# Adaptive-norm weights of the attention layer in 1 MB tiles of four row chunks, with their four products side by side

## The chip, the core and the metric

The kernel runs on one core of one Trainium2 chip. The metric is the device time of one execution in microseconds; the median of three runs of the kernel before is 3498.79 us (3496.82 to 3501.25).

## The reference, cut to what matters

Two blocks of two layers each are computed on 512 tokens of 1024 features, with 256 context tokens in the first block. In the first block every layer is steered by an adaptive norm:

```python
mod = jax.nn.silu(c) @ ada_w[i] + ada_b[i]            # [1, 6144]
sh1, sc1, g1, sh2, sc2, g2 = jnp.split(mod[:, None, :], 6, axis=-1)
mod_c = jax.nn.silu(c_ctx) @ ada_w[i] + ada_b[i]      # the same for the context
h = modulate(x, norm_mix_g[i], sh1, sc1)              # rmsnorm * (1 + sc) + sh
x = x + g1 * y                                        # y: attention (layer 0) or SSM (layer 1)
x = x + g2 * swiglu(modulate(x, norm_ffn_g[i], sh2, sc2), ...)
```

`ada_w` is [2, 1024, 6144] in float32, 24 MB a layer, and only two vectors (c and c_ctx) are multiplied with it.

## The kernel before, in words

The program is written for a tile framework: tiles come from pools with a fixed number of slots per tag, the framework sets all semaphores and orders each engine's instructions once, when the program is built, by their place in the program ("name@n" in an order gives way to n instructions) and by when they are expected to be ready. On the chip each engine then runs its list in that order.

**The adaptive norm.** `ada()` (line 434) makes 512 columns of mod at a time from `adal` (line 428), which holds silu(c) and silu(c_ctx) as two of 32 columns, for each of the eight row chunks. For chunk k it loads a [128, 512] tile `adaw` (256 KB, line 444, on the queue of SP) and multiplies (line 446): the 32 result rows go to the PSUM partitions 32 * (k % 4) and on, so chunks 0 to 3 write four different groups of 32 columns of the array, and chunks 4 to 7 add to the same four. Each such product in float32 is two MATMUL records in the trace. A copy by ACT (line 450, tile `adas`), four transposes on PE (line 452) and two short DVE instructions (lines 455 and 456) then give the columns in `mod`.

**Where it is called.** Tiles 0 to 3 of layer 0 are made at the start, two tiles at a time (phase "pre", 512 KB loads, eight slots). The other 20 tiles (line 2203, `rest`) are fillers of the attention of layer 0: `fill(n)` (line 2205), five for each of the four groups of heads, stands in the order `K["attn"]` as F.0 to F.4 between the steps Sc, S (scores and softmax), Vc, V (products with the values), P (preparing the next group's keys and queries) and o (output projection):

```python
rest = [(0, i) for i in range(4, 12)] + [(1, i) for i in range(12)]
def fill(n):
    l, i = rest[n]
    self.ada(l, [i], self.mod[l], (v1["ab0"], self.v2["ab1"])[l])
with self.side_pool("attnb") as ap:
    O = self.attn0(ap, op, qkv, xT, cT, m(2, 0), m(2, 1), fill)
```

`adaw` has six slots of 2 KB a partition there (`K["ada_w"]`, line 76), in the pool of the phase "attn". The pool "attnb" is opened at the other end of the memory, on the side where the pool of the normed activations `hx` and `hc` is closed just before (line 2200), with the pool "O" ahead of it; it holds the softmax's tiles `prob` (line 803). When attention is done it is closed, and `last_norm()` (line 2229) opens the pool of its tiles `h` on the same side.

**Other work beside it.** In a head group PE makes scores (lines 789, 790, 828, 830, 832), transposes of the exponentials (870), products with the values (883) and the turned reciprocals (895); DVE takes maxima (792, 850) and splits (312); ACT makes exponentials (799, 853) and splits (311). With the last group PE also makes the output projection's last part (lines 320 to 322, `g<-O,kwh`). SP's queue also loads the other weights (`wraw`, line 268), in the order of the list.

Of the kernel before, what the change touches and what calls it, by code (L numbers as in the profile page):

```python
# [9 lines left out]
F32 = mybir.dt.float32  # L10
# [18 lines left out]
# Choices: orders of issue, engines, numbers of slots and PSUM banks. In orders: steps "name", "name:lag" (of the group that many later) and "name@n" (gives way to n instructions).  # L29
# [46 lines left out]
    "ada_w": (6, 8),  # L76
# [29 lines left out]
class Act:  # L106
    """Feature-major activations split exactly into hi + lo: lists of [128, n] operands per chunk."""
# [5 lines left out]
class RmsStat:  # L113
    """Mean of squares of a token's features, gathered as the chunks [128, n] of x become final."""
# [33 lines left out]
class Gen:  # L148
# [11 lines left out]
    @contextmanager  # L160
    def phase(self, name, nc2, banks=(4, 2, 0, 0)):
        """A pool of one phase: nc2 general slots of [128, 512] and what else the phase allocates;
        banks: see banked()."""
        with self.tc.tile_pool(name=name, bufs=1, reuse_waits="tile") as p, ExitStack() as st:
            old = getattr(self, "ph", None), getattr(self, "nc2", 0)
            self.ph, self.nc2 = p, nc2
            if banks:
                st.enter_context(self.banked(name, *banks))
            yield p
            self.ph, self.nc2 = old  # L170

    @contextmanager
    def banked(self, name, *banks):
        """banks: slots of the PSUM tags "ps" (one bank), "ps2" (two banks), "S" and "F" (one bank)."""
# [7 lines left out]
    @contextmanager  # L182
    def kept_banks(self, **kept):
        """Banks that stay over phases, of the tags given."""
        with self.tc.tile_pool(name="ps_kept", bufs=1, space=PSUM, reuse_waits="tile") as q:
            self.kept = q, kept
            yield
            self.kept = None, {}

    def bank(self, tag, name):  # L190
        """The next bank of a tag, in turn those that stay and those of the phase."""
# [6 lines left out]
    def pipeline(self, order, n, call):  # L198
        """Issues the steps of n groups in the order given, as a software pipeline."""
# [15 lines left out]
    def schedule(self, order, calls):  # L215
        """Issues the steps "name.argument..." of an order."""
# [12 lines left out]
    def low(self, offset):  # L229
        """What is issued within gives way to the next `offset` instructions."""  # L230
        return self.tc.high_priority(offset=-offset)

# [31 lines left out]
    def wload(self, src, kc, cw):  # L264
        """src: DRAM AP [kc*128, cw]; returns the raw [128, kc, cw] view."""
# [5 lines left out]
    def wsplit(self, v, eng=None, early=False):  # L271
        """early: off the engines that finish what comes before."""
# [13 lines left out]
    def shift(self, key, g, dst, src, col):  # L286
        """dst = src + col, by the engine of a group."""
# [6 lines left out]
    def scale(self, key, g, dst, src, col):  # L294
        """dst = src * col, by the engine of a group."""
# [6 lines left out]
    def copy(self, key, dst, src):  # L302
        """dst = src, rounded to dst's type."""
# [5 lines left out]
    def split(self, hi, lo, src):  # L309
        """hi (f32r), lo (f32r) from an fp32 AP."""  # L310
# [3 lines left out]
    def mm3(self, ps, hv, lv, a, ks, first, last):  # L314
        """ps[128, n] += sum over ks of W_k^T a_k in three passes; hv[i], lv[i]: [128, 128]."""
# [8 lines left out]
    def mm3_cut(self, items, a, ks):  # L324
        """Products (ps, hv, lv) of all of a's tokens, the last 128 of them last, when they have been made."""
# [10 lines left out]
    def gemm(self, W, c0, nch, k0, kn, acts, epi, eng=None, ps=None, cut=0, early=0):  # L336
        """Output chunks c0/128 .. of W[k0*128:, c0:], for each of acts; epi(act index, chunk, psum AP).
        cut: so many chunks take the last 128 tokens last; early: of so many chunks, see wsplit()."""
# [24 lines left out]
    def columns(self, name, parts, slot=None, bank=None):  # L363
        """parts: list of (key, DRAM AP flat of n*128); returns dict key -> [128, n] columns."""
        return self.turned(name, bank, *self.rows(parts, slot))

    def rows(self, parts, slot=None, eng=None):
        """Loads the parts as rows."""
# [11 lines left out]
    def turned(self, name, bank, t, rows, where):  # L380
        """The columns of what rows() loaded."""
# [8 lines left out]
    def load_T(self, src, ntok, pool, name, eng):  # L390
        """[ntok, 1024] DRAM -> chunk APs [128, ntok] feature-major, in tiles of pool."""
# [33 lines left out]
    def ada_prep(self, *cols):  # L425
        """lhsT [128, 8, 32]: columns 0/1 are silu(c), silu(c_ctx)."""
# [7 lines left out]
    def ada(self, layer, tiles, mod, bcol):  # L434
        """mod [128, 48, 2] columns of silu(c) @ ada_w + ada_b, for tiles of 512 columns (one, or two next to each
        other); of the phase's tags "adaw" and "adas"."""
# [5 lines left out]
        for k in range(NK):  # L442
            v = self.ph.tile([P, n * 512], F32, tag="adaw", name="adaw", bufs=K["ada_w"][n - 1])
            nc.sync.dma_start(v, W[k * P:(k + 1) * P, tiles[0] * 512:(tiles[0] + n) * 512])
            for i in range(n):
                nc.tensor.matmul(ps[i][32 * (k % 4):32 * (k % 4) + 32, :], self.adal[:, k, :],
                                 v[:, i * 512:(i + 1) * 512], start=(k < 4), stop=(k >= 4))
# [10 lines left out]
    def gain(self, name, g, sc):  # L458
        """g * (1 + sc), [128, 8] columns."""
# [5 lines left out]
    def sums(self, ps, o, x, n, first, last):  # L465
        """Adds the sums over features of a chunk [128, n] to columns o.. of ps, one per 128 tokens."""
# [4 lines left out]
    def inv_root(self, ps, n, scale, eps):  # L471
        """(sums * scale + eps)^-0.5 as [128 tok, n/128]."""
# [7 lines left out]
    def bcast_cols(self, r, n, bank="ps"):  # L480
        """[128 tok, n/128] -> PSUM [128, n], the same row on every partition."""
# [6 lines left out]
    def new_act(self, nk, n, pool=None, tag=None, bufs=None):  # L488
        """Tiles of an Act; two chunks share a tile where n is 256."""
# [12 lines left out]
    def new_pair(self, n, pool, bufs):  # L502
        """An Act of two chunks, whose tiles are [128, 2, n] each (pair)."""
# [5 lines left out]
    def modnorm(self, chunks, n, A, sh, stat, act, pool=None):  # L509
        """rmsnorm * A + sh, split; pool: of what it needs."""  # L510
# [14 lines left out]
    def staggered(self, n, first, second, lag=1):  # L525
        """first(k) for k < n, each second(k, its result) `lag` steps later."""
# [7 lines left out]
    def resid(self, x, g, stats=None):  # L534
        """Epilogue: x_chunk += g * psum; stats gather the final chunks."""
# [8 lines left out]
    def swiglu(self, acts, x, g, wg, wu, wd, groups, last, mid=None):  # L544
        """last(k0, kn, hid) takes the last part of the last product."""
# [32 lines left out]
    def keep_weights(self, W, k0, kn, c):  # L578
        """W[k0*128:, c:c+512] split, in general slots: (hi, lo) [128, 512] per chunk."""
# [11 lines left out]
    def last(self, W, k0, kn, acts, x, g, stats, then):  # L591
        """x += g * product, first x, then ctx, with their stats; then(i) follows either."""
# [13 lines left out]
    def attn0_qkv(self, h, hc, wk, kps, kp):  # L606
# [27 lines left out]
        # keys [128 (2 heads), x 512] and [128 (2 heads), ctx 256] per pair of heads  # L634
# [18 lines left out]
        # values, token-major: [128 tok, chunk (x 4, ctx 2), kv head, hi 64 | lo 64]  # L653
# [18 lines left out]
        # queries as fp32 chunks  # L672
        qx, qc = {}, {}

        def prep(g, eng):
            # key stacks: rows 0:64 and 64:128 both hold the head; layout [ctx | x | ctx]
# [129 lines left out]
    def sink_sum(self, nm, psink, sm):  # L806
        """1 / (sm + exp(sink - max))."""
# [9 lines left out]
    def attn_block(self, q, khh, kll, k0, nk, g, masks, msk, nsink, psink):  # L817
# [17 lines left out]
        if nk > 512:  # L835
            # the fifth chunk of keys of all four heads
# [25 lines left out]
    def pv(self, Ps, rs, V, chs, g, O, n):  # L862
        """O^T of 4 heads: transposes of the exponentials, products with [vh | vl], halves added, rows scaled by rs."""
# [22 lines left out]
        # 1 / sum on the rows of its head  # L886
# [19 lines left out]
    def softplus_rows(self, dst, x, w):  # L906
        """dst = softplus(x), [r, n] fp32 APs on the same partitions; w: three scratch APs of that shape."""
# [4 lines left out]
        # log1p(u) = 2 atanh(s), s = u / (2 + u)  # L912
# [11 lines left out]
    def ssm(self, h, hc, x, g1, v2, cw, stat):  # L924
        nc, I = self.nc, self.I
# [11 lines left out]
        # half the convolution: silu(v) = u + u tanh(u), u = v / 2  # L937
# [7 lines left out]
        # token-major columns: [tok, chunk, 64] of -cum, dt, w; decay of each chunk on every partition  # L945
# [68 lines left out]
    def ssm_main(self, ph, h, hc, x, g1, v2, half, ncum, dtc, wtm, dd, scr, Dc, tri, stat):  # L1014
# [35 lines left out]
        def project_z(s, g, j):  # L1050
            """2 silu(z)"""
# [43 lines left out]
        def rows(s, g, c):  # L1095
            """Rows of cum of a chunk on every partition, both directions."""
# [8 lines left out]
        def states(s, g, d):  # L1105
            """Hs[d][c]: the state that chunk c starts from."""
# [28 lines left out]
        def products(s, g):  # L1135
            """C B^T, masked both ways."""
# [10 lines left out]
        def chunk(s, g, c):  # L1147
            i0 = c * P
            R = rows(s, g, c)
            # exponent: the smaller of both directions' (the other one is never below 0 there)  # L1150
# [27 lines left out]
        def finish(s, g):  # L1178
            """Skip, gate (doubled, and so is the norm's epsilon's root), group norm."""
# [26 lines left out]
    def final_norm(self, x, g, stat):  # L1206
        """x = rmsnorm(x) * g in place, and split."""
# [14 lines left out]
    def resid_alpha(self, x, first):  # L1222
        """Epilogue: x = ALPHA * x + psum for the first part of a product, x += psum for the others."""
# [7 lines left out]
    def mlp(self, act, x, w1, w2, groups, last):  # L1231
        """last(k0, kn, hid) takes the last part of the second product."""
# [18 lines left out]
    # S5: chunks of 4 tokens; states [128 = (2 groups, 64), 16 pairs of groups]  # L1251
    def cmul(self, eng, o, a, b, t):
        """o = a * b, complex: pairs (re, im) of APs; t: one scratch AP; o may not overlap a or b."""
# [8 lines left out]
    def exp_small(self, o, x, t):  # L1262
        """o = exp(x) of a few columns to float32's accuracy; t: scratch; o may be x."""
# [11 lines left out]
    def s5_tables(self, ph):  # L1275
        """In steps; sets self.tables."""
# [20 lines left out]
        # th modulo 2 pi, in three parts of 2 pi  # L1297
# [14 lines left out]
        # cos - 1 = -2 sin(r / 2)^2  # L1312
# [9 lines left out]
        # a - 1 = mag (cos - 1) + (mag - 1); mag - 1 = 2 t / (1 - t), t = tanh(lr dt / 2), where |lr dt| < 1  # L1322
# [14 lines left out]
        # (a - 1) / lam  # L1337
# [17 lines left out]
        # a^4 = r4 * w4; the turns w4^k  # L1355
# [5 lines left out]
        for i in range(8):  # L1361
            o = [col(f"s5p{i}r"), col(f"s5p{i}i")]
            self.cmul(nc.vector, o, pw[-1], pw[-1], t)
            # back to length 1
# [16 lines left out]
        # C a^tau, block-diagonal: [128 (g n), j, (tau, g, c)], im negated  # L1381
# [26 lines left out]
        # bbar and its powers a^tau bbar  # L1408
# [937 lines left out]
```

## Time and profile before

| | |
|---|---|
| median of three runs | 3498.79 us |
| span of the profiled execution (first to last instruction) | 3488.6 us |
| what lies around the span, against the median | 10.2 us |
| busy: PE, weight loads, DVE, ACT, POOL | 95%, 75%, 57%, 36%, 15% of the span |
| read from HBM | 285.30 MB, 83 GB/s over the span |
| attention of layer 0, from its first scores to the end of its last product | 149 to 508 us |

The profiled execution's own time is its span with some 10 us around it. A busy PE is one whose modelled matmuls cover the time; starts are measured, ends are modelled, so the cost of a matmul is read here from its start to the next instruction's start.

### The profile page before, as it was taken

To read this page: it belongs to the slowest core of one execution; us is meant where nothing else is said; L and a number is where in the kernel's file an instruction comes from. 1 tells how busy PE (TensorE), PEld (TensorE's weight loads), DVE (VectorE), ACT (ScalarE), POOL (GpSimd) and SP (SyncE) were. 2 spreads that over 40 slices of the span, in tenths; PEclk is the share of its full clock that TensorE was granted. 3 is DMA by queue.
4 is the path that set the end of the run, shared out by engine and by line. 5 is a ranking of instruction groups with operands and counts; after the bars stand their busy time and mean duration, and the time that the engine had idled before them with its cause. 6 is when DMAs were issued, how large, how long until landed. Compare 5 with 4: busy or idle time off the path is not lost. (4 is left out here: it accounts for less than half of the span.)

```text
span 3488.6 us, 43166 instructions
## 1 busy us (share of the span) xinstructions
PE 3326.3 (95%) x16689; PEld 2630.0 (75%) x16689; DVE 1998.7 (57%) x3596; ACT 1266.3 (36%) x2232; POOL 520.4 (15%) x647
## 2 busy tenths in 40 slices
PE   8989999999999999999899998999999988989999
PEld 6765558888887777777677876777888876778887
DVE  5476653333337777777854655655434469763335
ACT  4365522111224443333422323353322254652223
POOL 2232000000001443333210001311000022210000
PEclk9999999999999999999899999998999999999999
DMA  6314451222212322232123222312233332023332
GB/s 223 111 40 133 127 151 48 72 63 67 61 60 58 104 77 79 82 89 81 55 83 102 88 79 80 97 37 61 79 94 94 97 81 64 13 64 94 97 91 79
DMA packets 415405, 292.43 MB, mean 84 GB/s; under 512 B 16080, under 2 KB 374416, under 8 KB 415200
## 3 DMA queue, kind: packets, MB, share of 16 engines
q1 hardware_dynamic: 406864, 280.73, 27.2%
q10 hardware_dynamic: 6448, 6.10, 0.6%
q0 software_dynamic: 1888, 2.84, 0.3%
q8 instruction: 131, 2.15, 0.2%
q14 instruction: 74, 0.61, 0.1%
HBM read 285.30 MB, written 4.33 MB: 83 GB/s over the span
## 5 line engine op out<-in xcount | busy, mean ns | idle before, releaser
L282 ACT ACTIVATE whi<-wraw 128x1024 fp32r<-128x1024 f32 (+2 forms) x378 | 393.4, 1041 | 1039.4 <-PE g L321 888.0
L283 DVE TENSOR_TENSOR wlo<-wraw,whi 128x1024 fp32r<-128x1024 f32 (+2 forms) x336 | 406.7, 1211 | 437.9 <-ACT whi L282 436.3
L320 PE MATMUL g<-ah,whi 128*128 128x512 f32 (+1 forms) x1488 | 577.3, 389 | 6.8 <-DVE xT L537 3.3
L322 PE MATMUL g<-ah,wlo 128*128 128x512 f32 (+1 forms) x1488 | 575.6, 387 | 4.0 <-DVE wlo L283 2.1
L321 PE MATMUL g<-al,whi 128*128 128x512 f32 (+1 forms) x1488 | 575.0, 387 | 0.0
L322 PE MATMUL g<-h,wlo 128*128 128x512 f32 (+1 forms) x1296 | 458.5, 354 | 4.1 <-DVE wlo L283 3.6
L321 PE MATMUL g<-h,whi 128*128 128x512 f32 (+1 forms) x1296 | 458.6, 355 | 0.7 <-DVE h L520 0.7
L320 PE MATMUL g<-h,whi 128*128 128x512 f32 (+1 forms) x1296 | 456.6, 353 | 1.9 <-ACT whi L282 0.5
L320 PEld LDWEIGHTS g<-ah,whi 128*128 128x128 f32 x1488 | 282.2, 190 | 70.8 <-DVE xT L537 4.3
L322 PEld LDWEIGHTS g<-ah,wlo 128*128 128x128 f32 x1488 | 282.2, 190 | 66.9 <-DVE wlo L283 4.7
L321 PEld LDWEIGHTS g<-al,whi 128*128 128x128 f32 x1488 | 282.1, 190 | 61.6 <-DVE al L312 1.3
L322 PEld LDWEIGHTS g<-h,wlo 128*128 128x128 f32 x1296 | 245.1, 189 | 43.3 <-DVE wlo L283 6.5
L321 PEld LDWEIGHTS g<-h,whi 128*128 128x128 f32 x1296 | 245.1, 189 | 40.2 <-issue 3.8
L320 PEld LDWEIGHTS g<-h,whi 128*128 128x128 f32 x1296 | 245.1, 189 | 38.5 <-issue 2.7
L283 POOL TENSOR_TENSOR wlo<-wraw,whi 128x1024 fp32r<-128x1024 f32 x48 | 115.5, 2407 | 818.6 <-ACT whi L282 815.5
L320 PE MATMUL g<-act,whi 128*128 128x512 f32 x568 | 225.9, 398 | 2.4 <-ACT qk L1873 2.4
L322 PE MATMUL g<-act,wlo 128*128 128x512 f32 x568 | 225.5, 397 | 1.5 <-POOL wlo L283 1.5
L321 PE MATMUL g<-act,whi 128*128 128x512 f32 x568 | 225.5, 397 | 0.0
L537 DVE SCALAR_TENSOR_TENSOR xT<-g,mod,xT 128x512 f32<-128x512 f32 x184 | 137.2, 748 | 111.0 <-PE g L322 109.0
L320 PEld LDWEIGHTS g<-act,whi 128*128 128x128 f32 x568 | 107.5, 189 | 28.3 <-ACT qk L1873 2.6
L322 PEld LDWEIGHTS g<-act,wlo 128*128 128x128 f32 x568 | 107.2, 189 | 27.8 <-POOL wlo L283 1.8
L321 PEld LDWEIGHTS g<-act,whi 128*128 128x128 f32 x568 | 107.2, 189 | 25.6
(724 smaller groups left out, 5865.5 us busy)
## 6 DMA issues: line engine op xcount, KB each, us to landing
wraw<-in_mlp_w_dram SPq DMA_DIRECT2D x128, 512.0 KB, 4.1
adaw<-in_ada_w_dram SPq DMA_DIRECT2D x160, 256.0 KB, 3.1
wraw<-in_ssm_w_in_dram SPq DMA_DIRECT2D x49, 512.0 KB, 4.0
wraw<-in_ffn_w_gate_dram SPq DMA_DIRECT2D x44, 512.0 KB, 3.9
wraw<-in_ffn_w_up_dram SPq DMA_DIRECT2D x44, 512.0 KB, 3.8
R<-cumscr SPq DMA_DIRECT2D x64, 256.0 KB, 4.2
wraw<-in_ffn_w_down_dram SPq DMA_DIRECT2D x28, 512.0 KB, 3.4
adaw<-in_ada_w_dram SPq DMA_DIRECT2D x16, 512.0 KB, 7.8
```

The lines of the kernel that those rows point to most:

```text
L282: self.nc.scalar.activation(hv, v, AF.Copy)
L283: (eng or self.nc.vector).tensor_tensor(lv, v, hv.bitcast(F32), op=OP.subtract)
L320: nc.tensor.matmul(ps, hv[i], a.hi[k], start=f, stop=False)
L321: nc.tensor.matmul(ps, hv[i], a.lo[k], start=False, stop=False)
L322: nc.tensor.matmul(ps, lv[i], a.hi[k], start=False, stop=l)
L537: self.nc.vector.scalar_tensor_tensor(x[ai][c], ps, g[ai][:, c:c + 1], x[ai][c], op0=OP.mult, op1=OP.add)
```

## The change

`ada()` for one tile of 512 columns (the fillers) loads four row chunks with one transfer into a tile [128, 4, 512], 1 MB, then issues its four products one behind the other; so two transfers a tile of columns in place of eight. The tag has two slots (16 KB a partition) in place of six of 2 KB, and the fillers' tiles come from the pool "attnb". For pairs of tiles (the start) nothing changes. Elsewhere the diff only takes away comments and docstrings.

```diff
-    "ada_w": (6, 8),
+    "ada_w": (2, 8),
...
-    def ada(self, layer, tiles, mod, bcol):
+    def ada(self, layer, tiles, mod, bcol, pool=None):
...
-        for k in range(NK):
-            v = self.ph.tile([P, n * 512], F32, tag="adaw", name="adaw", bufs=K["ada_w"][n - 1])
-            nc.sync.dma_start(v, W[k * P:(k + 1) * P, tiles[0] * 512:(tiles[0] + n) * 512])
-            for i in range(n):
-                nc.tensor.matmul(ps[i][32 * (k % 4):32 * (k % 4) + 32, :], self.adal[:, k, :],
-                                 v[:, i * 512:(i + 1) * 512], start=(k < 4), stop=(k >= 4))
+        per = 4 if n == 1 else 1
+        for k0 in range(0, NK, per):
+            v = (pool or self.ph).tile([P, per, n * 512], F32, tag="adaw", name="adaw", bufs=K["ada_w"][n - 1])
+            nc.sync.dma_start(v, W[k0 * P:(k0 + per) * P, tiles[0] * 512:(tiles[0] + n) * 512]
+                              .rearrange("(k p) c -> p k c", p=P))
+            for k in range(k0, k0 + per):
+                for i in range(n):
+                    nc.tensor.matmul(ps[i][32 * (k % 4):32 * (k % 4) + 32, :], self.adal[:, k, :],
+                                     v[:, k - k0, i * 512:(i + 1) * 512], start=(k < 4), stop=(k >= 4))
...
-                    self.ada(l, [i], self.mod[l], (v1["ab0"], self.v2["ab1"])[l])
+                    self.ada(l, [i], self.mod[l], (v1["ab0"], self.v2["ab1"])[l], self.ap)
```

## Rows read from the trace of the kernel before

**Rows 1.** The page's first part: busy us (share of the span) xinstructions.

```profile
PE 3326.3 (95%) x16689; PEld 2630.0 (75%) x16689; DVE 1998.7 (57%) x3596; ACT 1266.3 (36%) x2232; POOL 520.4 (15%) x647
```

**Rows 2.** Busy time by stretch of the attention; then PE's clock, DMA share, GB/s.

```profile
150.00:192.00 42.00, 39.92 (x200) 18.95 (x198) 26.85 (x69) 25.14 (x69) 13.54 (x17) 1.00 0.63 201
192.00:268.00 76.00, 67.51 (x386) 50.49 (x386) 62.34 (x149) 53.00 (x148) 19.71 (x27) 0.98 0.04 11
268.00:319.00 51.00, 50.58 (x218) 20.59 (x218) 26.01 (x67) 23.96 (x59) 10.50 (x14) 1.00 0.64 200
319.00:357.00 38.00, 36.31 (x211) 27.74 (x209) 32.80 (x76) 23.42 (x64) 9.90 (x12) 1.00 0.12 38
357.00:407.00 50.00, 49.77 (x223) 20.60 (x222) 24.20 (x69) 21.50 (x55) 3.97 (x5) 1.00 0.65 202
407.00:449.00 42.00, 41.22 (x245) 32.53 (x244) 33.91 (x82) 23.26 (x66) 4.60 (x5) 1.00 0.12 36
449.00:508.00 59.00, 58.31 (x233) 23.33 (x230) 26.73 (x57) 16.63 (x31) 0.00 (x0) 1.00 0.71 214
```

**Rows 3.** Sum of the same stretches for line 446 (the fillers' products) alone.

```profile
sum 358.00, PE 105.24 PEld 14.83; mean PE 15.03 PEld 2.12
```

**Rows 4.** PE, 150 to 508 us: products of line 446 and the row behind.

```profile
150.22 0.64 PE L446 MATMUL ada<-adaw,adal 128*32 128x512 f32 x4
...
150.22 1.91 PE L446 MATMUL ada<-adaw,adal 128*32 128x512 f32 x12
152.06 0.39 PE L789 MATMUL S<-khh,qsc 128*128 128x256 f32 x1
...
159.52 1.05 PE L446 MATMUL ada<-adaw,adal 128*32 128x512 f32 x4
160.50 0.50 PE L883 MATMUL po<-pl,V 128*128 128x512 f32 x1
...
162.62 1.04 PE L446 MATMUL ada<-adaw,adal 128*32 128x512 f32 x2
163.59 0.51 PE L883 MATMUL po<-pl,V 128*128 128x512 f32 x1
...
310.46 1.06 PE L446 MATMUL ada<-adaw,adal 128*32 128x512 f32 x6
311.45 0.33 PE L870 MATMUL pT<-ident,prob 128*128 128x128 f32 x1
...
507.10 1.05 PE L446 MATMUL ada<-adaw,adal 128*32 128x512 f32 x2
```

**Rows 5.** Waits around the fillers: total us, times, longest us.

```profile
PE ada L446 <- DMA adaw<-in_ada_w_dram: 2.2, 3, 1.5
...
SPq L444 <- PE ada L446: 157.6, 79, 26.4
```

**Rows 6.** Start of the attention, PE and ACT, in order of time.

```profile
149.06 0.28 PE L322 MATMUL g<-hc,wlo 128*128 128x256 f32 x1
...
155.25 0.44 PE L870 MATMUL pT<-ident,prob 128*128 128x128 f32 x2
...
154.14 0.47 ACT L799 ACTIVATE prob<-S,nm 128x256 f32<-128x256 f32 x1
```

**Rows 7.** The page's DMA issues: count, KB each, median us to landing.

```profile
wraw<-in_mlp_w_dram SPq DMA_DIRECT2D x128, 512.0 KB, 4.1
adaw<-in_ada_w_dram SPq DMA_DIRECT2D x160, 256.0 KB, 3.1
...
wraw<-in_ffn_w_down_dram SPq DMA_DIRECT2D x28, 512.0 KB, 3.4
adaw<-in_ada_w_dram SPq DMA_DIRECT2D x16, 512.0 KB, 7.8
```

**Rows 8.** All DMA between 52 and 56 us, a stretch with its queues full.

```profile
DMA packets 861, 1.51 MB, mean 377 GB/s; under 512 B 95, under 2 KB 162, under 8 KB 860
```

**Rows 9.** ACT's first norm behind the attention.

```profile
514.53 2.04 ACT L516 ACTIVATE h<-nt,mod 128x512 fp32r<-128x512 f32 x3 [5.38 <-DVE nt L515]
```

## The prediction

> **What bounds the kernel now.** I read the page's busy shares first: PE is busy for 95% of the span and nothing else comes near [rows 1]. So the change counts by what it does to PE's list. All it touches lies in the attention of layer 0, so next I read the busy time by stretch there [rows 2]. Four stretches have fillers (150 to 192, 268 to 319, 357 to 407, 449 to 508 us; 202 us together): their DMA runs at 200 GB/s, PE is busy for 198.6 us, and DVE for only 104 us. The three stretches between (156 us) have almost no DMA, PE is busy for 145.0 us, DVE for 129 us (83%). The fillers' products alone cover 105 us of PE [rows 3], half of the stretches that hold them. In those, time is PE's time, and the question is what the products cost in PE's list and what would end waits if they cost less.
>
> The timeline of PE answers the first half [rows 4]. A product (two records) that stands alone between other work holds PE from 162.62 to 163.59, 0.97 us. Two side by side, from 159.52 to 160.50, 0.98 us. Three, from 310.46 to 311.45, 0.99 us. Six, four column groups and then two of them again, 1.84 us. So neighbours in other column groups are nearly free, and a lone product wastes the room of three. Last, the waits: PE waited for the fillers' data only 2.2 us in all, while SP's queue waited 157.6 us for PE to give slots back [rows 5]. Data is early now; slots are what loads wait for.
>
> **The change, part by part.** *Removed.* From the first to the last product of the fillers [rows 4] I count 95 bursts: 59 lone products at 0.975, 24 pairs at 0.98, 5 triples at 0.99, 4 sixes at 1.84, and three mixed ones at 1.44, 2.40 and 2.14 us, which is 57.5 + 23.5 + 5.0 + 7.4 + 6.0 = 99.4 us. One more product ran alone during the Q projections, 0.97 us. Sum 100.4 us, in line with the 105.24 us of modelled busy time [rows 3], which counts each burst's overlapped end as well.
>
> *Added.* 40 groups of four. No burst of just four products is in the trace. Below, it costs what three cost, 0.99 us; above, two pairs one after the other, 1.96 us. I take 1.0 us: in the view cut off at 150.65 us the first four records of the six have started by then and end within 0.64 us, and the six, four and then two, need 1.84 us where a pair alone needs 0.98 [rows 4]. So the four add 0.86 us, or about 1.0 us alone with the change to other work. That makes 40 us, and 60 us less on PE.
>
> The rows show that three neighbours cost 0.99 us where one costs 0.97, so 2.9 times the throughput [rows 4]. The Trainium skill, "TensorE: Matmul & The Clock Gate", section "Part 3: Packing small matmuls — row/col tiling", says less: 2.38 times for three column tiles, 3.07 for four row tiles. By 3.07 a group of four would be an estimated 1.27 us the gross gain 49 us in place of 60 and the time 3466 us (fifth rival). The trace disagrees for three (2.9), so the sum goes by the trace.
>
> The DMA issues fall from 160 to 40 on SP's queue. SP is not on the path and I put nothing down for that. Copy, transposes and DVE work of each tile stay as they are, and 20 of them are spread as before.
>
> *Given back at the start.* At 150 us PE used the wait for the first softmax for fillers whose data had been loaded 100 us earlier. The first exponentials run at 154.14, and PE's transposes of them at 155.25 [rows 6]. The new tiles lie where the Q projections' input lay, so the first 1 MB cannot be asked for much before their last product at 149.06 [rows 6], and arrives after this hole. Filler time that ran in the hole saved nothing by leaving: 4 us (bounds: 0, if other work fills it, and 5.2 us, all bursts up to 160 us).
>
> *Given back to the softmax.* The stretches without fillers have PE idle for 11.0 of 156 us, 7%; those with fillers for 3.4 us [rows 2], on 97 us of other work. With 60 us of cover gone, I let that other work idle at the same 7%: 7 us, so 4 more than now. Bounds 0 and 8 us (11% as in 192 to 268).
>
> *Given back to late transfers.* Other work in the filler stretches is 97 us, 2.4 us for each of the 40 groups; if the order keeps that spacing, a group comes every 3.4 us, and one of the two slots has 2 x 3.4 - 1.0 = 5.8 us between its release and its next use. A transfer of 256 KB landed after 3.1 us; 512 KB after 3.4 to 4.1; 512 KB in a crowd after 7.8 [rows 7]. Continuing the step from 256 to 512 KB, 1 MB lands after 4.0 to 6.1 us; twice the crowded value, 15.6 us, is the upper bound. The rate asked for is 1 MB in 3.4 us, 308 GB/s, where a full queue moved 377 [rows 8]. So the slots come back just in time. I take 0.2 us late per group, 8 us in all; nothing below, and above the case of the first rival.
>
> The 3.1 us of a 256 KB transfer [rows 7] is from issue to landing. The Trainium skill, "DMA: Bandwidth & Descriptors", section "Anatomy of one DMA — SWDGE (gpsimd) path", gives about 2.0 us plus bytes over 436 GB/s for the other issuing path; an estimate by it is 4.4 us for 1 MB, and the late transfers would cost nothing, a gain of 52 us and 3447 us. For 256 KB it gives 2.6 us where the trace has 3.1, so it looks somewhat early here.
>
> *Sum.* 60 - 4 - 4 - 8 = 44 us. The profiled span would go from 3488.6 to about 3445 us. The median stands 10.2 us above the span of the profiled run, by what lies around it, and goes from 3498.8 to 3455 us.
>
> **The rivals.** A measurement of this kernel can tell about 0.2%, 7 us, from no change.
>
> *First: late transfers (chance 0.20).* Two slots are shallow where six were deep. If 1 MB lands after 7 us in place of 5.8, each slot is 1.2 us late, 0.6 us per group, 24 us in all; at 8 us 44 us are lost. The deciding point is 5.8 us. For it: the crowded 7.8 us, and that DMA share is already 0.63 to 0.71 in these stretches [rows 2, 7]. Against it: the queue can move 377 GB/s [rows 8]. With 24 us lost the gain is 60 - 8 - 24 = 28 us, with 44 us it is 8; middle 18 us, 3481 us.
>
> *Second: the softmax chain takes over (chance 0.09).* With PE shorter, DVE and ACT pace the heads. DVE has 233 us in these 358 us [rows 2]. At the forecast's 314 us that is 74%, below the 81 to 86% that it keeps in the stretches without fillers; against the rival. If it keeps no more than 70%, the stretch takes 333 us, a gain of 25 us: 3474 us.
>
> *Third, slower: the four are not neighbours (chance 0.05).* If PE's order puts other work between the four products of a tile, each stands alone again: 160 x 0.975 = 156 us against 100.4, 56 us slower, 3555 us. It is slower from 103 bursts on. Against it: what had been loaded ahead ran in sixes without a break, four times [rows 4]. For it: thirteen products came in mixed bursts, some with waits inside.
>
> *Fourth: the new place of the tiles (chance 0.07).* SP's queue is in order: a 1 MB load that waits for the Q projections' input, or for a slot, holds the weights behind it; and the tiles of the norm behind the attention (first written at 514.53 [rows 9]) are laid over the fillers' and must wait for the last of them. It decides if the last group runs after the last output projection. It would cost the gain of the last stretch and perhaps of the first, 25 to 50 us: no change or nearly, 3495 us.
>
> *Fifth: four overlap less than three (chance 0.03).* If the array took three at once and the fourth behind them, four would cost as the six do, 1.84 us [rows 4], 34 us more in all: a gain of 10 us, 3489 us. Against it: the start of the six. The 3.07 cited above would be a milder form of it.
>
> **How the numbers follow.** The forecast has 0.56; its own range, with all small terms at their bounds (none of them: 59 us; at worst 5 + 8 + 16 us off 60, so 31), is 3440 to 3468. The 80% range takes in the second rival and most of the first: 3437 to 3489. Faster by more than 7 us: the forecast, the second rival, 0.17 of the first, and 0.02 each of the fourth and fifth, 0.86. Within: 0.03 of the first, 0.02 of the fourth and 0.01 of the fifth, 0.06. Slower: the third and 0.03 of the fourth, 0.08.
>
> **What would show it.** Right: some 40 bursts of eight records of line 446, 1.0 us each, and about 43 us of busy time in place of 105; filler stretches at 280 to 310 GB/s and some 40 us in all shorter; everything behind the attention unchanged and only earlier. Late transfers show as PE waiting for adaw's DMA, far over 2.2 us; the second rival as PE waiting for ACT and DVE in these stretches; the third as lone pairs of records; the fourth as a later first norm or weights. The prediction is wrong if a burst of four costs far more than 1.0 us, or if the time saved between 150 and 508 us is not there at the end.

## The result, and the profile after

The changed kernel has a median of 3463.01 us (3455.86 to 3465.07, four runs) against 3497.81 us (3493.56 to 3501.25, four runs) for the one before on the same chip: ratio 0.9891, 95% interval 0.9876 to 0.9907, 34.8 us faster. The forecast was 3455 us, its own range 3440 to 3468. The profiled execution took 3465.07 us with a span of 3463.2 us. Lines behind the changed loop have moved by four: the fillers' products are line 450 now.

The page's busy times, in the columns of [rows 1]: PE lost 42.6 us and is still busy for 95% of the span.

```profile
PE 3283.7 (95%) x16689; PEld 2637.0 (76%) x16689; DVE 2001.2 (58%) x3596; ACT 1266.0 (37%) x2232; POOL 516.8 (15%) x647
```

Busy time by stretch of the attention, in the columns of [rows 2], cut where stretches with and without fillers meet now; the second fence is the sum for the fillers' products alone, as in [rows 3].

```profile
150.00:196.00 46.00, 38.42 (x208) 19.91 (x207) 27.34 (x72) 27.53 (x78) 13.37 (x17) 0.93 0.61 203
196.00:273.00 77.00, 68.55 (x393) 51.73 (x391) 63.26 (x155) 53.91 (x146) 21.72 (x30) 0.98 0.04 15
273.00:307.00 34.00, 31.17 (x206) 16.80 (x206) 23.50 (x61) 22.83 (x56) 9.75 (x13) 1.00 0.84 280
307.00:351.00 44.00, 41.63 (x244) 32.66 (x245) 38.57 (x91) 26.74 (x78) 8.78 (x12) 1.00 0.14 48
351.00:384.00 33.00, 29.91 (x200) 16.04 (x198) 23.04 (x60) 18.75 (x47) 3.73 (x4) 1.00 0.82 267
384.00:427.00 43.00, 41.47 (x243) 32.54 (x243) 33.17 (x79) 22.73 (x60) 4.66 (x5) 1.00 0.20 65
427.00:467.00 40.00, 34.41 (x212) 18.63 (x212) 23.22 (x50) 14.02 (x27) 0.00 (x0) 0.97 0.91 289
sum 317.00, PE 285.56 PEld 188.31 DVE 232.10 ACT 186.51 POOL 62.01; mean PE 40.79 PEld 26.90 DVE 33.16 ACT 26.64 POOL 8.86
```

```profile
sum 317.00, PE 46.86 PEld 7.20; mean PE 6.69 PEld 1.03
```

Where 358 us stood, 317 stand, 41 us less. PE's busy time fell by 58.1 us (343.6, the sum of [rows 2], to 285.6), which is the fillers' products (105.24 to 46.86). PE's idle time rose by 17.1 us, from 14.4 to 31.4. In stretches with fillers it rose from 3.4 to 19.1 us: in the first from 2.1 to 7.6, in the two middle ones from 0.7 to 5.9 together, in the last from 0.7 to 5.6. Between them it hardly rose (11.0 to 12.4). The second and third filler stretch shrank from 51 and 50 to 34 and 33 us, the last from 59 to 40; the first grew from 42 to 46.

Three places of PE's timeline (as in [rows 4]; in brackets the idle time ahead of a row and what ended it): the start of the attention, two bursts of its second stretch, and its end.

```profile
149.94 0.28 PE L794 MATMUL S<-kll,qsc 128*128 128x256 f32 x1
154.19 0.69 PE L874 MATMUL pT<-ident,prob 128*128 128x128 f32 x2 [3.98 <-ACT prob L803]
...
156.01 1.94 PE L450 MATMUL ada<-adaw,adal 128*32 128x512 f32 x8
157.88 1.33 PE L874 MATMUL pT<-ident,prob 128*128 128x128 f32 x5
...
273.56 1.92 PE L450 MATMUL ada<-adaw,adal 128*32 128x512 f32 x16 [0.30 <-DVE xT L541]
275.41 0.50 PE L887 MATMUL po<-pl,V 128*128 128x512 f32 x1
...
281.07 1.07 PE L450 MATMUL ada<-adaw,adal 128*32 128x512 f32 x8
282.07 0.66 PE L874 MATMUL pT<-ident,prob 128*128 128x128 f32 x4
...
457.94 1.06 PE L450 MATMUL ada<-adaw,adal 128*32 128x512 f32 x8
458.94 0.38 PE L322 MATMUL g<-O,kwl 128*128 128x256 f32 x1
...
461.04 1.07 PE L450 MATMUL ada<-adaw,adal 128*32 128x512 f32 x8 [0.60 <-DMA adaw<-in_ada_w_dram]
465.04 1.94 PE L450 MATMUL ada<-adaw,adal 128*32 128x512 f32 x8 [2.93 <-DMA adaw<-in_ada_w_dram]
467.75 1.12 PE L456 MATMUL adat<-ident,adas 128*128 128x128 f32 x4 [0.78 <-ACT adas L454]
468.66 3.41 PE L472 MATMUL st<-ones,sq 128*128 128x1 f32 x16
```

A group of four is one row of eight records and costs 1.00 us (281.07 to 282.07), two groups in a row 1.85. Of 39 bursts 30 are one group, 4 are two groups; the other five are pieces of two groups in the first stretch.

The end is what [rows 4] had not shown: two groups run behind the last output projection (458.94), each after a wait for its transfer, and the sums of squares for the next norm (`st`) stand behind them, 9.7 us after that product. In the kernel before they followed 2.5 us after the last product:

```profile
506.89 0.28 PE L322 MATMUL g<-O,kwl 128*128 128x256 f32 x1
...
509.38 1.84 PE L468 MATMUL st<-ones,sq 128*128 128x1 f32 x16
...
515.30 0.80 PE L320 MATMUL g<-h,whi 128*128 128x512 f32 x1
```

Waits of PE and of SP's queue, columns as in [rows 5]; then the fillers' tile: SP's issues (count, min/median/max ns, first and last start) and the time to landing, which answer to [rows 7].

```profile
PE ada L450 <- DMA adaw<-in_ada_w_dram: 5.9, 5, 2.9
PE S L832 <- ACT prob L857: 4.5, 7, 2.0
PE adat L456 <- ACT adas L454: 4.2, 6, 1.2
PE pT L874 <- ACT prob L803: 4.0, 1, 4.0
...
SPq L446 <- PE ada L450: 95.2, 28, 30.6
```

```profile
L446 SPq DMA_DIRECT2D adaw<-in_ada_w_dram x40: 367/368/499, 144.6 to 459.1; - x40
...
DMA to landing us min/median/max: 5.1/5.2/8.3
```

PE waited for the fillers' data 5.9 us, not tens of microseconds, and 3.5 of them are the two waits of the end. The last transfer was issued at 459.1, when the group of 457.94 had freed its slot; its products began at 465.04.

**From the attention to the end.** The first product of the next feed-forward starts 39.16 us earlier (515.30 to 476.14), and its first down projection too (604.93 to 565.79). The two profiled spans differ by 25.4 us only, the medians by 34.8. The runs below say where the rest is.

### The profile page after: what moved, and what is told of

The parts are those of the page before. It is cut to its first block, busy times and chain, and to the rows that moved or that the text cites. A ratio compares the mean times of both kernels' runs of the same rounds, so it can differ in the third digit from the quotient of the medians.

```text
span 3463.2 us, 42928 instructions
## 1 busy us (share of the span) xinstructions
PE 3283.7 (95%) x16689; PEld 2637.0 (76%) x16689; DVE 2001.2 (58%) x3596; ACT 1266.0 (37%) x2232; POOL 516.8 (15%) x647
## 5 line engine op out<-in xcount | busy, mean ns | idle before, releaser
L320 PE MATMUL g<-h,whi 128*128 128x512 f32 (+1 forms) x1296 | 457.7, 354 | 1.4 <-ACT whi L282 0.5
```

Source lines behind the costliest of these rows:

```text
L320: nc.tensor.matmul(ps, hv[i], a.hi[k], start=f, stop=False)
```

## The experiments

Each ratio below is against executions of the kernel before that ran beside that experiment; medians of different experiments come from different chips, so they are compared by these ratios. Times in this table are starts on PE in each profiled execution (us): the first scores, the last `g<-O,kwh` product of the output projection, the first product of the feed-forward; then the differences, of which the last is called the tail.

| kernel | scores | last product | feed-forward | scores to last | last to feed-forward |
|---|---|---|---|---|---|
| before | 149.2 | 506.8 | 515.3 | 357.6 | 8.5 |
| before, again | 149.1 | 506.0 | 514.5 | 356.9 | 8.5 |
| after | 148.6 | 457.7 | 476.1 | 309.1 | 18.4 |
| after, again | 145.9 | 453.8 | 472.0 | 308.0 | 18.2 |
| two column groups | 148.3 | 487.5 | 494.6 | 339.2 | 7.0 |
| 22 general slots | 146.9 | 455.3 | 472.6 | 308.3 | 17.3 |
| 22 and three fillers' slots | 147.7 | 452.7 | 461.0 | 305.0 | 8.3 |
| 22 and the old pool | 153.5 | 456.3 | 474.1 | 302.8 | 17.8 |
| F.3 without lag | 147.0 | 457.9 | 466.4 | 310.9 | 8.5 |

**Both kernels once more.** No edit.

> The changed kernel once more. In its first trace the FFN behind the attention started 39.2 us earlier than before, but the end came only 25.4 us earlier: 10 us went between 1182 and 1697 us and 5 us after 3067 us. Theory: those 14 us are differences between two executions, not the change; then the FFN starts at 476 us within 1.5 us again, and the SSM stretch takes a different time, with a ratio of medians of 0.988 to 0.991. Rival: the change slows the later stages (other places in memory); then the same 10 us and 5 us are missing again.

> The kernel before once more, for a second trace. Theory of differences between executions: the attention's end and the FFN's start stand at 515 us within 1.5 us, and the stretch from 1182 to 1697 us differs from the first trace by several us. Rival (the later stages are slowed by the change): that stretch takes 515.4 us within 2 us as in the first trace.

Measured: 3456.23 us (3452.78 to 3457.65) against 3497.56, ratio 0.9883 (0.9868 to 0.9898), 41.3 us; the one execution of before took 3497.15 us with a span of 3495.4. The feed-forward started at 472.03 where I expected 476; 2.8 us of that lie ahead of the attention, whose first scores came earlier. From the scores to the feed-forward the two pairs of traces agree: 366.1 to 327.5 and 365.5 to 326.2, 38.6 and 39.3 us less. Behind it the first trace of before was the odd one. Its SSM stretch (1181.8 to 1697.2) took 515.4 us; the second trace of before needed 522.3, the two of after 525.2 and 523.3. So what was lost behind the attention in the first pair is a difference between executions; the last section shows what kind.

**Four transfers of 256 KB into the 1 MB tile.** Place, size and number of the tiles stay, only the transfer is cut.

```diff
-            nc.sync.dma_start(v, W[k0 * P:(k0 + per) * P, tiles[0] * 512:(tiles[0] + n) * 512]
-                              .rearrange("(k p) c -> p k c", p=P))
+            for k in range(per):
+                nc.sync.dma_start(v[:, k, :], W[(k0 + k) * P:(k0 + k + 1) * P, tiles[0] * 512:(tiles[0] + n) * 512])
```

> The four products stay neighbours, but the 1 MB tile is filled by four transfers of 256 KB. Theory that neighbours on PE make the gain: line 446's work still takes some 40 bursts of 1.0 us, the FFN starts within 3 us of 476 us, a ratio of 0.988 to 0.992. Rival that the larger transfer makes it (fewer issues, better rate): 160 issues are back, landing is later, and 10 us or more of the gain are lost (FFN at 486 us or later).

Measured: 3505.05 us, ratio 1.0021 (1.001 to 1.0031), 7.5 us slower than before. My expectation of 40 bursts fell: there are 95, of 103.9 us. PE's timeline shows one tile's products apart again:

```profile
284.43 1.04 PE L450 MATMUL ada<-adaw,adal 128*32 128x512 f32 x2
285.41 0.39 PE L793 MATMUL S<-khh,qsc 128*128 128x256 f32 x1
...
286.42 1.05 PE L450 MATMUL ada<-adaw,adal 128*32 128x512 f32 x4
287.40 0.44 PE L874 MATMUL pT<-ident,prob 128*128 128x128 f32 x2
```

Each product's own load is expected at another time, and the framework orders PE's list by such times; so other work slips in between. This is the third rival of the prediction, produced by an edit. It also shows what place and two slots do in this order: nothing gained, and the feed-forward 11.8 us later (527.07), of which one wait of PE for the residual's last chunk (`cT`) takes 9.5. The list now has output-projection products behind `st`, and DVE makes the norm's `nt` and `h` (514.2 to 525.1 us) before it comes to this `cT`.

**The same four transfers, products held together.** The product of the last quarter is issued first, the other three right behind it.

```diff
+            def product(k, i):
+                return nc.tensor.matmul(ps[i][32 * (k % 4):32 * (k % 4) + 32, :], self.adal[:, k, :],
+                                        v[:, k - k0, i * 512:(i + 1) * 512], start=(k < 4), stop=(k >= 4))
+            if n == 1:
+                ins = product(k0 + per - 1, 0)
+                with self.tc.issue_after(ins.ins):
+                    for k in range(k0, k0 + per - 1):
+                        product(k, 0)
```

> Four transfers of 256 KB again, but the four products are held together: the one of the last quarter is issued first and the other three are ordered right behind it. Theory that neighbours on PE make the gain, and the one transfer only because all four are then ready at once: 40 bursts or fewer as in the changed kernel, the FFN starts at 462 to 478 us, ratio 0.984 to 0.990. Rival that the large transfer itself is worth something: the FFN starts at 486 us or later, ratio over 0.993.

Measured: 3463.19 us, ratio 0.9896 (0.9875 to 0.9918), 40 bursts of 46.1 us. With the same transfers as the run above it takes 41.9 us less, and equals the change. From the scores to the first down projection it takes 417.5 us, the run above 465.7, the change 417.2 and 415.8 in its two traces. So the gain is the neighbours', not the larger transfer's. The tails differ: here, as in the run above, one wait for `cT` (8.4 us) stands ahead of the feed-forward, where the change has its two late groups. In PE's timeline a group is one row again:

```profile
283.93 1.06 PE L449 MATMUL ada<-adaw,adal 128*32 128x512 f32 x8
284.93 0.50 PE L894 MATMUL po<-pl,V 128*128 128x512 f32 x1
```

**Two column groups in place of four.** The 1 MB transfers stay; four products go to two groups of columns, so two stand side by side and two follow.

```diff
+        g = 2 if n == 1 else 4
-                    nc.tensor.matmul(ps[i][32 * (k % 4):32 * (k % 4) + 32, :], self.adal[:, k, :],
-                                     v[:, k - k0, i * 512:(i + 1) * 512], start=(k < 4), stop=(k >= 4))
+                    nc.tensor.matmul(ps[i][32 * (k % g):32 * (k % g) + 32, :], self.adal[:, k, :],
+                                     v[:, k - k0, i * 512:(i + 1) * 512], start=(k < g), stop=(k >= NK - g))
...
-            nc.scalar.activation(sb, ps[i], AF.Copy)
+            nc.scalar.activation(sb[:32 * g], ps[i][:32 * g], AF.Copy)
```

The copy, the transposes and the sum behind them shrink to two groups as well.

> As the changed kernel, but the four products use two column groups instead of four, so that they run as two pairs one after the other (copy and transposes of 64 rows instead of 128). Theory that PE's list sets the time: a burst takes 1.84 us in place of 1.0 us, 40 bursts cost 34 us more, and at least 24 us of it arrive (FFN at 500 us or later; ratio about 0.996 to 0.999). Rival that the DMA or the softmax already paces the filler stretches: less than 15 us arrive (FFN before 491 us).

Measured: 3479.2 us, ratio 0.9949 (0.9934 to 0.9963); 40 bursts of 76.1 us in all against 52.1, a group now 1.84 us:

```profile
287.88 1.91 PE L451 MATMUL ada<-adaw,adal 128*32 128x512 f32 x8
289.72 0.50 PE L888 MATMUL po<-ph,V 128*128 128x512 f32 x1
```

The feed-forward came at 494.6, 18.4 and 22.5 us later than in the two traces of after: between my two expectations. The table says why. Up to the last product the stretch is 30 us longer. Of the 52.1 us in the change's bursts 7.7 lie behind that product, waits among them; ahead of it they take 44.4, here 76.1, and these 31.7 us are what the stretch grew by. So up to there the time follows the cost of the bursts, as PE's list has them. But the tail is 11 us shorter: with slower groups the transfers come in time, and nothing is left behind the output projection.

**Three slots.** Room for the third 1 MB tile comes from four general slots fewer (22, not 26), so a control has those 22 alone.

```diff
-    "ada_w": (2, 8),
-    "attn_c2": 26,
+    "ada_w": (3, 8),
+    "attn_c2": 22,
```

> The changed kernel with 22 general slots in place of 26 in the attention, which makes room for the next two. Both theories: nothing else changes much; the FFN starts between 470 and 479 us, ratio 0.987 to 0.991.

> As the control, with three 1 MB slots in place of two. Theory that two slots hold the fillers back at the end (the last 1 MB was asked for at 459 us, when the slot came free, and PE then stood for 3.5 us in all and ran at half clock): the last transfers are asked for one group earlier, the FFN starts 4 to 9 us earlier than in the control. Rival that the transfer rate paces the last stretch (DMA share 0.91 there): less than 2 us.

Measured: control 3447.84 us (3444.92 to 3456.75), ratio 0.986 (0.9843 to 0.9877); three slots 3445.54 (3438.19 to 3446.58), ratio 0.9845 (0.983 to 0.986). The control's attention is that of after, to within about 1 us in the last two columns; its ratio is a little under the 0.987 that I expected at the least. With three slots the tail shrinks from 17.3 to 8.3 us, and the feed-forward starts 11.7 us earlier, more than the 4 to 9 expected. SP asks for the last tile at 445.3 us now, and the end of PE's timeline is like that of before, at full clock (`st` 1.84 us):

```profile
451.13 1.06 PE L450 MATMUL ada<-adaw,adal 128*32 128x512 f32 x8
453.03 1.06 PE L450 MATMUL ada<-adaw,adal 128*32 128x512 f32 x8
454.88 0.66 PE L456 MATMUL adat<-ident,adas 128*128 128x128 f32 x4 [0.78 <-ACT adas L454]
455.37 1.84 PE L472 MATMUL st<-ones,sq 128*128 128x1 f32 x16
```

In the medians only 2.3 us of the 11.7 show, and the intervals overlap; that three slots make the whole faster is not shown.

**The last filler earlier.** In the order of steps F.3 runs one group late, so the last group's F.3, one tile or two groups of four, stands behind everything. Without the lag it stands among the output projection.

```diff
-        "Sc.0 F.1 Sc.1 F.0 S.0@400 F.2 Vc.0 Vc.1 S.1 F.3:-1 P:1 V.0 S.2 V.1 F.4 S.3 V.2 V.3 o.0@400 o.1@400",
+        "Sc.0 F.1 Sc.1 F.0 S.0@400 F.2 Vc.0 Vc.1 S.1 F.3 P:1 V.0 S.2 V.1 F.4 S.3 V.2 V.3 o.0@400 o.1@400",
```

> The changed kernel with F.3 in place of F.3:-1 in the order, so that the four filler stretches have five tiles each instead of 4, 5, 5 and 6. Theory that the last stretch has more to load than it has time for: its 12 MB become 10 MB, the stats of the norm start within 3 us of the last output projection (10.9 us in the changed kernel), and the FFN starts 4 to 9 us earlier than 472 to 476 us. Rival that what is taken from the last stretch comes back in the first: less than 2 us.

Measured: 3445.44 us, ratio 0.9851 (0.9836 to 0.9866). `st` starts 2.5 us behind the last `g<-O,kwh` product, the tail is 8.5 us as before, the feed-forward at 466.4. Some 2 to 3 us come back ahead of it: from the scores to the last product it takes 310.9 us, in the two traces of after 309.1 and 308.0. The same loss is mended without a third slot, so it was the place of the last tile in PE's list together with its late transfer.

**The old pool.** The fillers' two 1 MB slots lie in the pool of the phase again, where the first transfer need not wait for the Q projections' input.

```diff
-                    self.ada(l, [i], self.mod[l], (v1["ab0"], self.v2["ab1"])[l], self.ap)
+                    self.ada(l, [i], self.mod[l], (v1["ab0"], self.v2["ab1"])[l])
```

> As the control, with the 1 MB tiles in the pool of the phase, as before the change, so that the first two can be loaded during the Q projections. Theory that the new place costs the start (PE waits 4.0 us for the first softmax and falls to half clock): the first burst stands at 150 to 152 us instead of 156, PE's wait for the first exponentials shrinks by 2 us or more, and the scores of the second head group (203 us before, 204 after) start 3 to 6 us earlier than in the control. Rival that the softmax alone makes the hole: less than 1.5 us there.

Measured: 3456.74 us, ratio 0.9879 (0.9863 to 0.9896). The hole at the start closes: fillers run at 154.53, and PE waits 1.2 us for the first exponentials in place of 4.0.

```profile
154.53 1.92 PE L450 MATMUL ada<-adaw,adal 128*32 128x512 f32 x14
...
159.03 0.44 PE L874 MATMUL pT<-ident,prob 128*128 128x128 f32 x2 [1.22 <-ACT prob L803]
```

From the scores to the last product it takes 302.8 us, 5.5 less than the control; one of the fillers' products, 1.0 us, has moved ahead of the scores, so the hole's price is some 4.5 us. The scores of the second head group come 50.9 us behind the first ones, in the control 54.9, within the 3 to 6 us expected, but counted from the execution's start they come 2.6 us later. For the first scores start 6.6 us later: that product runs among the projections ahead of them (at 85.90 us), and there PE waits 2.5 us for a split weight (`v` for `whi`), which the control's trace does not have, with a granted clock of 0.89 between 60 and 90 us where the control has 1.00, 3.3 us more. No net gain.

**Three slots and no lag.** Both mends together, with 22 general slots.

> Three slots and F.3 without its lag together, with 22 general slots. Theory that both mend the same thing (fillers that come after the last output projection): no more than 4 us better than three slots alone, the FFN starts at 456 to 462 us, ratio 0.983 to 0.986. Rival that they mend different things and add up: the FFN starts at 455 us or earlier.

Measured: 3439.95 us (3438.93 to 3445.05), ratio 0.9842 (0.9823 to 0.986). The feed-forward's first product starts at 457.19, within the 456 to 462 expected of mends for one thing, but in this order some feed-forward products stand ahead of the context's sums, so the first down projection is the fairer mark. It starts at 551.23, with three slots alone at 550.58: both mends cure one thing, and don't add up. These three (three slots, no lag, both) are the fastest of the study, 0.984 to 0.985 of before, where the change has 0.988 to 0.989; since the control with 22 slots stands at 0.986, their lead over the change is shown in the traces (7 to 13 us from the scores to the first down projection), and in the whole only roughly.

## Why the prediction was right

**Removed and added: right.** 60 us were forecast for PE, 58.1 came [rows 2, 3], the fillers' products at 46.9 us of busy time in place of some 43. A burst of just four, which no row of before showed, costs 1.00 us, the value taken between 0.99 and 1.96; the run with two column groups shows what four cost as two pairs, 1.84. In throughput that is 3.9 times a lone product (4 x 0.97 over 1.00), and the fifth rival, 1.84 us a group, falls with it. The Trainium skill, "TensorE: Matmul & The Clock Gate", section "Part 3: Packing small matmuls — row/col tiling", gives 3.07 times for four row tiles and has no row for four column tiles; four column tiles here do better than that.

**Given back: 16 forecast, 17.1 measured, but not where I put it.** *The start*, 4 us: the hole is there, 3.98 us ahead of the first transposes, and the first group comes at 156.01. What I left out: PE's granted clock fell to half behind the hole (0.93 over the stretch, some 3 us), so with both the first stretch gained nothing. *The softmax*, 4 us: too small. Of the 17.1 us, 4.0 are the hole and 3.7 the fillers' data (waits of 2.2 us before, 5.9 after); that leaves 9.4, of which 1.4 in the stretches without fillers and the rest in those with fillers, for the most part short waits for ACT and DVE, the second rival in a small form: for `adas`, say, 4.2 us where the kernel before had 1.0. *Late transfers*, 0.2 us a group, 8 us in all: too large, 3.7 in place of 8, and this is the step that failed in its form. That 16 and 17.1 lie so close is luck: one term was too small by 5 us, another too large by 4. 1 MB landed after 5.2 us, within the 4.0 to 6.1 taken and under the deciding 5.8, and the middle groups waited 1.4 us in all. By the Trainium skill, "DMA: Bandwidth & Descriptors", section "Anatomy of one DMA — SWDGE (gpsimd) path", whose rule is for the other issuing path, an estimate was 4.4 us; the trace has it later. The loss lies at the end, where the last tile stands behind the output projection: two slots and 5.2 us let its transfers start too late, and the tail grew from 8.5 to 18.4 us. The fourth rival had named this point ("if the last group runs after the last output projection"), but for other reasons, memory and SP's queue, and at 25 to 50 us; it is about 10. Three slots and the order without lag each take it back. Whether the norm's sums are held by their place in PE's list alone, or also by the PSUM banks that they share in turn with the fillers, I did not try.

**What lies around the span: wrong.** I took 10.2 us from the median less one span. The profiled executions stand 1.8 to 1.9 us above their spans (3465.07 and 3463.2; 3497.15 and 3495.4), not some 10 us as the section on the profile before has it. The rest must be that the traced execution of before was faster than its median; its own time is not on record. It did not change the forecast, which went by differences.

**The sum.** 44 us were forecast. At the attention's end it is 41 us, at the feed-forward 39 (the tail at half clock). The medians give 34.8 and 41.3 us in the two comparisons; the traces suggest that what lies between them is what differs from one execution to the next behind the attention. Two steps of the range are loose: with none of the terms given back the sum is 60 us, not 59, and the 16 us that it allows late transfers have no working; at the sum's 8 us it would have ended at 3460, short of the 3463 measured.

## What to carry to other kernels

Products with few columns of weights are worth ordering so that they stand side by side in PE's list: four cost what one costs, and what keeps them together is that they become ready at one time (one transfer, or an order by hand), not the size of the transfer. Large tiles with few slots need a look at the last of them: count back from its use by the landing time and the slot's release, and see what stands behind it in the list. And work that fills a wait saves nothing when it is made cheaper or moved away: find such waits first, and don't count that work into the gain.

## What the runs showed of the hardware that I had not expected

**The clock behind a wait.** Granted clock by stretch (third number from the end), after the change: behind the 4.0 us wait at the start, and behind the 2.9 us wait of the end, it fell to half, 1.2 in place of 2.4 GHz. The sums of squares took 3.41 us there where they took 1.84 before.

```profile
152.00:156.00 4.00, 1.80 (x7) 1.34 (x7) 0.77 (x6) 3.31 (x10) 0.19 (x1) 0.71 0.11 41
156.00:160.00 4.00, 4.00 (x17) 2.00 (x16) 2.02 (x7) 1.29 (x3) 0.41 (x1) 0.50 0.21 37
...
459.00:467.00 8.00, 3.98 (x23) 0.93 (x21) 0.84 (x3) 1.01 (x2) 0.00 (x0) 0.83 1.08 315
467.00:476.00 9.00, 6.88 (x32) 6.76 (x32) 1.84 (x6) 1.23 (x2) 1.03 (x1) 0.50 0.25 60
```

In the kernel before, fillers ran in the same wait at the start, and the clock stayed:

```profile
156.00:160.00 4.00, 4.00 (x27) 1.97 (x25) 2.59 (x10) 3.20 (x14) 0.41 (x1) 1.00 0.92 322
...
3121.80:3129.80 8.00, 7.46 (x62) 7.05 (x61) 2.77 (x4) 3.82 (x6) 0.00 (x0) 1.00 0.01 4
3129.80:3137.80 8.00, 8.00 (x36) 6.44 (x35) 4.93 (x7) 4.24 (x6) 0.00 (x0) 1.00 0.47 131
```

**The same wait, with and without a drop.** The last two of these rows are a place far behind the change; here it is in the profiled execution after:

```profile
3091.20:3099.20 8.00, 7.46 (x49) 7.06 (x49) 2.37 (x3) 3.82 (x6) 0.00 (x0) 0.80 0.01 4
3099.20:3107.20 8.00, 8.00 (x29) 6.85 (x29) 3.95 (x6) 2.80 (x4) 0.00 (x0) 0.56 0.43 119
```

PE is idle for 0.54 us in both, but in one execution the clock drops behind it, and some 4.8 us are lost there (by the starts of the same products before and behind it). Such drops can be summed from the feed-forward to the end, as time multiplied by one less the granted clock. They take 85.5 us in the first trace of before, 94.4 in the second, 99.2 and 94.1 in the two of after, 79.0 in the control with 22 slots, 84.8 with three slots. Without them the six stretches take 2886 to 2892 us. So nearly all of the 13.8 us that the first pair of traces loses between the feed-forward and the end go with the clock (13.7); in the second pair the drops are equal, and the stretch is 3.0 us longer. The control's short time is of the same kind, and so are the 5 us that the three slots lose on it behind the attention (5.8 us more of drops). What decides whether the clock drops at such a place, and whether the number of slots has a part in it, stays open.
